# Second attention with its maps combined on VectorE, norm weights in the split, last transpositions among the projections, and zero products in four places

## The chip, the cores and the metric

The kernel runs on one core of a Trainium2 chip. The metric is the time of one execution on the device in microseconds (us); the median of several runs counts. Five engines work beside each other, each through its own queue of instructions in order: TensorE (PE: matrix products and transpositions), VectorE (DVE), ScalarE (ACT), GpSimd (POOL) and SyncE (SP), which here only issues DMAs. They wait for each other by semaphores.

## What is computed

Two transformer blocks on 256 tokens of width 1024 in float32. The change lies in the first half of the first block, whose second attention is a differential one: two softmax maps per head, the second subtracted with a weight, and a norm over each head's output:

```python
def _diff_attend(q, k, v, lam):
    s = jnp.einsum('bqhmd,bkhmd->bhmqk', q, k).astype(jnp.float32) * (HEAD_DIM ** -0.5)
    p = jax.nn.softmax(s, axis=-1)
    a = (p[:, :, 0] - lam * p[:, :, 1]).astype(v.dtype)
    return jnp.einsum('bhqk,bkhe->bqhe', a, v)

def _diff_out(o, subln, lam_init):
    o = _rmsnorm(o, subln, SUBLN_EPS) * (1.0 - lam_init)
    return o.reshape(o.shape[0], o.shape[1], B_WIDTH)

def _merge(ya, yb, ga, gb, w_oa, w_ob, w_out):
    merged = jax.nn.sigmoid(ga) * (ya @ w_oa) + jax.nn.sigmoid(gb) * (yb @ w_ob)
    return merged @ w_out

# in first_block, x: 256 tokens, ctx: 256 more keys and values
        ya = _sweep_query_blocks(_gqa_attend, qa, ka_all, va_all)
        yb = _sweep_query_blocks(lambda qq, kk, vv: _diff_attend(qq, kk, vv, lam), qb, kb_all, vb_all)
        yb = _diff_out(yb, subln_b[l], lam_init)
        x = x + g_a * _merge(ya, yb, ga, gb, w_oa[l], w_ob[l], w_out[l])
        ...
        x = x + g_m * moe(hx.reshape(b * s, d)).reshape(b, s, d)
```

There are 4 heads with two maps each, 512 keys, and a value width of 128; `lam_init` is 0.2, so the norm's weight is multiplied by 0.8. Attention A has 8 query heads over 2 key heads. `moe` has 32 experts of which each token takes four. The second block (three more attentions and a feed-forward layer) follows.

## The kernel before

**Products in float32.** A dense product is made of three fast ones: both operands are split into a high part, rounded to the fast format, and a low part, the rest. For weights `ensure_split` does it a quarter of a tile at a time: ScalarE writes `wh` (L316), VectorE writes `wl` (L319). `dense_tok` (L354 to L356) and `dense_feat` (L388 to L390) use them. `split_out` (L508) splits results for the next product, with an optional scale.

**Weights.** All weights come as tiles of 1 MB in one list; `fill` issues their DMAs on SP's queue as soon as a slot of the ring is free, `free` releases a slot when its last reader is done. In the first block the list also holds 16 tiles `("ada", g, k)` of the modulation's weights. `ada_one` (L659) multiplies such a tile with a column on VectorE and adds it up in `ga_b` and `gm_b` (L667 and L669); after eight tiles it has the sums over partitions made by TensorE (L676), copies them to `mrow` (L679) and transposes them (L682 and L689).

**Order.** The program is written as a foreground (the dense products, a quarter after the other) and a list `bg` of small tasks, of which `pump` runs some after each quarter: the norms of keys and queries, the steps of `attend_a` and `attend_b`. The compiler's scheduler then orders each engine's queue by its own estimates; so the order on an engine is not quite that of the text.

**First steps.** The modulation's first part is made by `ada_first` and `ada_second`: `mrow` (L640), two transpositions (L646), `mod` (L650), `ab`. With it `feat_norm` makes the normalised input `hi_t`, `lo_t` from transpositions of `xn` (L467); `warm` puts zero products between (L556).

**Attention A**, 16 units: scores (`mm3_pair`, L362), `soft` with exponential on ScalarE (L878) and a scaling by GpSimd (L900), `trans` (L910), product with the values (L922). It is spread over the projections `vb` and `g1`.

**Attention B**, 8 units of two maps each, over the projection `g1`: after the second map's exponential GpSimd multiplies it with 1/sum and -lambda (L962), VectorE scales the first and adds (L963), TensorE transposes (L971), multiplies with the values (L983), ScalarE copies the result to `va_sb` (L986). When all are done, `fin1` makes the norm: squares on ScalarE (L1007), sums (L1008), a reciprocal root in 13 small steps (`rsqrt`, L404 to L423), two multiplications by it (L1012) and two by the norm's weights `subln` (L1013), all on VectorE; `fin2` transposes (L1019) and splits into `yb`.

**Output.** The products with `w_oa` and `w_ob` (key `oab`, L1177 to L1179) take two quarters of `ya` and two of `yb` for each half; after the first quarter rows are spread over all partitions (`spreads`). Then `w_out` (`wo`), the residual `x_sb` (L1245), its transpositions for the router (L467), the router (L1233), the choice of experts on VectorE, and the experts (`expert_mm`, L1431) with up to 19 slots for their tiles. `keep_warm` (L447) puts products without use between.

## Time and profile before

| | us |
|---|---|
| median of 3 runs | 1687.87 (1687.73 to 1687.89) |
| profiled execution | 1689.61 |
| its span | 1687.7 |
| TensorE busy | 1627.8 (96%) |
| VectorE busy | 693.5 (41%) |
| ScalarE busy | 465.6 (28%) |
| GpSimd busy | 84.0 (5%) |

The profiled execution is one of its own; the durations come from it, and what lies outside its span is 1.9 us. By stage: the first 296 us are the first block's modulation, projections, attentions and router, with attention A from about 116 to 167 us and B from there to 217 us; from 296 to about 1240 us the experts; then the second block. A row of the timeline gives start, duration, engine, line, operation, written tile, read tiles, shape, and in brackets the idle time of the engine just before and what ended it. TensorE's clock is given as the share of 2.4 GHz that was granted.

### The profile page before, as it was taken

Reading aid. Unit: us, or ns where it says so; the run is one execution under the profiler, and the core shown is the slowest. Engines: PE = TensorE matmul, PEld = TensorE weight load, DVE = VectorE, ACT = ScalarE, POOL = GpSimd, SP = SyncE. Lnnn points to the kernel's source line nnn. Section 1 sums busy time; section 2 is a strip of 40 time slices with the busy share of each in tenths; the row PEclk is TensorE's granted clock in tenths of the full one; section 3 lists DMA queues with packets and bytes.
Section 4 is the critical chain, followed back from the end, with each engine's and each line's share of the span. In section 5 each row is a group of like instructions: output and inputs, shape, how many; then the busy total and the mean of one; then the engine's idle time right before and its main releaser. Section 6 shows DMA issues by size and latency. Waiting matters only on the chain. (4 is left out here: it accounts for less than half of the span.)

```text
span 1687.7 us, 22284 instructions
## 1 busy us (share of the span) xinstructions
PE 1627.8 (96%) x9091; PEld 1021.4 (61%) x9091; DVE 693.5 (41%) x1352; ACT 465.6 (28%) x769; POOL 84.0 (5%) x116
## 2 busy tenths in 40 slices
PE   8999999999999999899999999999999999999997
PEld 5877887444433443354344334434488899989996
DVE  4998986211111111121221111111367556665555
ACT  3435563101000100010001001000256445454443
POOL 3012200000000000000000000000004101100000
PEclk9999999999999999999999999999999999999999
DMA  9654669899999999999999999999973433565540
GB/s 380 240 193 157 203 243 371 368 425 426 425 425 425 425 425 426 384 425 425 426 425 426 425 425 426 426 408 425 405 291 108 142 123 128 179 217 183 174 158 25
DMA packets 117155, 537.29 MB, mean 318 GB/s; under 512 B 11882, under 2 KB 13622, under 8 KB 66874
## 3 DMA queue, kind: packets, MB, share of 16 engines
q1 hardware_dynamic: 112160, 532.19, 78.9%
q10 hardware_dynamic: 4458, 3.46, 0.6%
q8 instruction: 72, 1.18, 0.3%
q14 instruction: 33, 0.27, 0.0%
q0 software_dynamic: 432, 0.19, 0.0%
HBM read 534.75 MB, written 1.05 MB: 317 GB/s over the span
## 5 line engine op out<-in xcount | busy, mean ns | idle before, releaser
L1431 PE MATMUL bank_a<-w,xg 128*64 128x512 f32 x2048 | 521.9, 598 | 1.1 <-DMA w<-in_w_up_dram 1.1
L1431 PEld LDWEIGHTS bank_a<-w,xg 128*64 128x64 f32 x2048 | 184.7, 137 | 276.7 <-issue 254.0
L319 DVE TENSOR_TENSOR wl<-w,wh 128x1024 fp32r<-128x1024 f32 (+1 forms) x193 | 236.6, 1231 | 154.3 <-ACT wh L316 144.0
L316 ACT ACTIVATE wh<-w 128x1024 fp32r<-128x1024 f32 (+1 forms) x193 | 202.0, 1049 | 217.2 <-PE bank_a L389 88.2
L1431 PE MATMUL bank_a<-w,at 128*64 128x512 f32 x960 | 228.0, 595 | 6.2 <-DVE e L1462 5.3
L390 PE MATMUL bank_a<-hi,wl 128*128 128x256 f32 x640 | 180.3, 283 | 1.0 <-DVE wl L319 1.0
L388 PE MATMUL bank_a<-hi,wh 128*128 128x256 f32 x616 | 176.3, 287 | 1.1 <-ACT hi L474 0.6
L389 PE MATMUL bank_a<-lo,wh 128*128 128x256 f32 x616 | 174.3, 283 | 0.2 <-DVE lo L475 0.2
L1431 PEld LDWEIGHTS bank_a<-w,at 128*64 128x64 f32 x960 | 83.7, 137 | 145.6 <-issue 104.4
L513 ACT ACTIVATE y<-bank_a,ws 128x512 fp32r<-128x512 f32 x32 | 22.0, 688 | 441.6 <-PE bank_a L1431 431.7
L390 PEld LDWEIGHTS bank_a<-hi,wl 128*128 128x128 f32 x640 | 122.3, 192 | 1.4 <-DVE wl L319 1.4
L388 PEld LDWEIGHTS bank_a<-hi,wh 128*128 128x128 f32 x616 | 117.8, 192 | 3.2 <-issue 0.9
L389 PEld LDWEIGHTS bank_a<-lo,wh 128*128 128x128 f32 x616 | 118.1, 192 | 0.9 <-DVE lo L475 0.6
L514 DVE SCALAR_TENSOR_TENSOR y<-bank_a,ws,y 128x512 fp32r<-128x512 f32 x32 | 24.0, 751 | 217.1 <-ACT y L513 215.5
L1462 DVE TENSOR_SCALAR e<-bank_a 128x512 f32<-128x512 f32 x32 | 22.1, 691 | 187.3 <-PE bank_a L1431 185.7
L1452 ACT ACTIVATE e<-gs 128x512 f32<-128x512 f32 x32 | 20.2, 631 | 236.5 <-DVE gs L1451 224.9
L1341 PEld LDWEIGHTS bank_a<-gr,x_sb 128*128 128x128 f32 x512 | 65.1, 198 | 22.7 <-issue 19.5
L1451 DVE TENSOR_SCALAR gs<-bank_a 128x512 f32<-128x512 f32 x32 | 22.1, 692 | 134.4 <-PE bank_a L1431 114.1
L1341 PE MATMUL bank_a<-gr,x_sb 128*128 128x128 f32 x512 | 70.2, 289 | 0.2 <-DVE gr L1324 0.2
L1346 DVE TENSOR_SCALAR xg<-bank_a,abp 128x128 f32<-128x128 f32 x64 | 22.0, 404 | 107.8 <-PE bank_a L1341 107.6
L1349 ACT ACTIVATE xg<-bank_a,abp 128x128 f32<-128x128 f32 x64 | 24.3, 456 | 122.7 <-PE bank_a L1341 122.6
L354 PE MATMUL bank_b<-wh,hh 128*128 128x512 f32 x128 | 49.9, 390 | 0.0
(468 smaller groups left out, 2215.6 us busy)
## 6 DMA issues: line engine op xcount, KB each, us to landing
w<-in_w_up_dram SPq DMA_DIRECT2D x144, 1024.0 KB, 19.5
w<-in_w_down_dram SPq DMA_DIRECT2D x136, 1024.0 KB, 19.5
w<-in_w_gate_dram SPq DMA_DIRECT2D x128, 1024.0 KB, 18.5
w<-in_w_in_dram SPq DMA_DIRECT2D x44, 1024.0 KB, 7.4
w<-in_w_ada_dram SPq DMA_DIRECT2D x16, 1024.0 KB, 5.6
w<-in_w_ada_dram SPq DMA_DIRECT2D x16, 512.0 KB, 8.9
w<-in_w_out_dram SPq DMA_DIRECT2D x8, 1024.0 KB, 8.4
w<-in_w_down_dram SPq DMA_DIRECT2D x16, 512.0 KB, 10.9
```

The lines of the kernel that those rows point to most:

```text
L316: split_last[0] = S.activation(r32(wh[:, :n]), t[:, o:o + n], AF.Copy)
L319: V.tensor_tensor(r32(wl[:, :n]), t[:, o:o + n], wh[:, :n], op=OP.subtract)
L354: PE.matmul(o, r32(sh), r32(mh), start=first, stop=False)
L388: PE.matmul(o, r32(wh[:, k, c]), r32(hi[:, j]), start=j == 0 and m % 2 == 0, stop=False)
L389: PE.matmul(o, r32(wh[:, k, c]), r32(lo[:, j]), start=False, stop=False)
L390: PE.matmul(o, r32(wl[:, k, c]), r32(hi[:, j]), start=False, stop=j == 7 and m % 2 == 1)
L514: V.scalar_tensor_tensor(out=r32(lo), in0=src, scalar=scale, in1=hi, op0=OP.mult, op1=OP.subtract)
L1341: PE.matmul(ps[:, k], x_sb[:, tt, o:o + 255:2], d["gr"][:, tt].rearrange("p e s -> p (e s)"), start=tt == 0, stop=tt == 1)
L1349: S.activation(xg[:, j], ps[:, k], AF.Identity, bias=abp_[:, 1, j:j + 1], scale=abp_[:, 0, j:j + 1])
L1431: state["mm"] = PE.matmul(ps[h][64 * ab:64 * ab + 64], lhs(j, ab), w[ab][:, e, 512 * h:512 * h + 512], start=bias is None and j == 0, stop ...
L1451: V.tensor_scalar(out=g_, in0=ps[h], scalar1=7.0, scalar2=None, op0=OP.min)
L1462: V.tensor_scalar(out=u_, in0=ps[h], scalar1=7.0, scalar2=-7.0, op0=OP.min, op1=OP.max)
```

## The change

- **Attention B.** GpSimd's scaling is gone. With both sums known, VectorE takes the reciprocals of both at once and makes one column, -lambda times first sum over second sum; one operation over 512 columns adds the second map times this column to the first. The missing 1/(first sum) is the scale of ScalarE's copy of the product with the values. Squares are summed there too, per head and half of the tokens, by a ScalarE operation over 128 columns.
- **Its norm** is made in two parts: heads 0 to 2 in the last step but one, head 3 as the last task, each with its own 13 small steps. The weights `subln` are a column now, loaded as an 81st row of `rows` and turned with these; they are the scale in `split_out`.
- **Last transpositions** stand after the first quarter of `oab`, the spreads after the second.
- **Attention A** has two empty tasks more ahead of its first transposition, and 15 zero products (`warm_tile`) on TensorE just before it.
- **`ada_one`**: what follows the copy to `mrow` is a task of its own (`ada_rest`), at most one task later.
- **Zero products**: 16 instead of 8 at the start, 7 between two pairs of transpositions of `x_sb`, 14 instead of 8 ahead of the choice of experts.

```diff
-    def transposed(ps, j0, src):
-        for k in range(2):
-            for tt in range(2):
-                turned[tt] = PE.transpose(ps[:, k, 128 * tt:128 * tt + 128], src[:, tt, 128 * (j0 + k):128 * (j0 + k) + 128], ident)
+    def transposed(ps, j0, src, mid=None):
+        for k, tt in ((0, 0), (1, 0), (0, 1), (1, 1)) if mid else ((0, 0), (0, 1), (1, 0), (1, 1)):
+            if mid and (k, tt) == (0, 1):
+                mid()
+            turned[tt] = PE.transpose(ps[:, k, 128 * tt:128 * tt + 128], src[:, tt, 128 * (j0 + k):128 * (j0 + k) + 128], ident)
...
+        nc.gpsimd.dma_start(out=rows[80:81], in_=I["subln_b"])
...
+        def warm_tile(t, n, inst):
+            with tc.issue_after(inst.ins):
+                for _ in range(n):
+                    PE.matmul(t, zero_b[:, 0:128], zero_b, start=True, stop=True)
...
             V.tensor_copy(mrow, ps)
+            bg.insert(min(len(bg), 1), lambda: ada_rest(g, mrow))
+
+        def ada_rest(g, mrow):
             pt = bank("b", shape=(128, 4, 128))
...
-        warm(8, turned[1])
+        warm(16, turned[1])
...
                 pt = bank("b", shape=(128, 4, 128))
+                if u == 0:
+                    warm_tile(pt[:, 0:2].rearrange("p a n -> p (a n)"), 15, pair_last[0])
...
-            return [step(n) for n in range(21)]
+            return [step(n) for n in range(3)] + [lambda: None] * 2 + [step(n) for n in range(3, 21)]
...
-                    G.tensor_scalar(out=pr, in0=pr, scalar1=rl, scalar2=nlam, op0=OP.mult, op1=OP.mult)
-                    V.scalar_tensor_tensor(out=p0, in0=p0, scalar=r0, in1=pr, op0=OP.mult, op1=OP.add)
+                    p0 = st[u][1]
+                    V.reciprocal(rinv[:, u], mx[:, 2:6:3])
+                    V.scalar_tensor_tensor(out=mx[:, 6:7], in0=mx[:, 2:3], scalar=nlam, in1=rinv[:, u, 1:2],
+                                           op0=OP.mult, op1=OP.mult)
+                    V.scalar_tensor_tensor(out=p0, in0=pr, scalar=mx[:, 6:7], in1=p0, op0=OP.mult, op1=OP.add)
...
-                S.copy(late["sb"][:, qt, h], ps)
+                S.activation(late["sb"][:, qt, h], ps, AF.Copy, scale=rinv[:, u, 0:1])
+                S.activation(sqj, late["sb"][:, qt, h], AF.Square, accum_out=bss[:, h // 3, qt, h % 3:h % 3 + 1])
...
+            def norm(k):
+
+                n = (3, 1)[k]
+                hs = slice(3 * k, 3 * k + n)
+
+                def run():
+                    r = rsqrt(bss[:, k, :, 0:n], (2, n), 1.0 / 128, 1e-5)
+                    for qt in ((0, 1), (slice(0, 2),))[k]:
+                        y = late["sb"][:, qt, hs]
+                        rr_ = r[:, qt].unsqueeze(2 if k == 0 else 3)
+                        V.tensor_tensor(y, y, rr_.to_broadcast([128, n, 128] if k == 0 else [128, 2, n, 128]), op=OP.mult)
+                return run
...
-                    split_out(late["yb"][:, 0, :, s], late["yb"][:, 1, :, s], pt)
-                return run
-            late["fin"] = [fin2(0), fin2(1)]
-            return [step(n) for n in range(23)] + [fin1, lambda: None, late['fin'][0], late['fin'][1]]
+                split_out(late["yb"][:, 0, :, s], late["yb"][:, 1, :, s], pt, subln)
+            late["fin"] = fin2
+            tasks = [step(n) for n in range(23)]
+            tasks[21] = seq2(tasks[21], norm(0))
+            return tasks + [norm(1)]
...
-        subln = p1.tile([128, 128], F32, name="subln")
+        subln = p1.tile([128, 1], F32, name="subln")
...
+        V.tensor_scalar(out=subln, in0=cols[:, 96:97], scalar1=0.8, scalar2=None, op0=OP.mult)
...
             ada_one()
+        flush()
...
                 if (h, q) == (0, 0):
+                    late["fin"](0)
+                    late["fin"](1)
+                if (h, q) == (0, 1):
                     for f in spreads:
                         f()
...
-                    transposed(ps, 4 * h + 2 * b, x_sb)
+                    transposed(ps, 4 * h + 2 * b, x_sb, (lambda: keep_warm(7, turned[0])) if h and not b else None)
...
-        keep_warm(8, routed)
+        keep_warm(14, routed)
```

The scheduler moves instructions at more places than the text does. In the order listings below a row gives line, operation, written tile, read tiles and shape; lines of the changed kernel are 2 to 41 higher than those of before.

VectorE at the second half of `ada_first`, where `mod` (L650 before, L660 after) is waited for by TensorE's transpositions of `xn`. Before:

```order
L1053 TENSOR_TENSOR sgn<-rope,gains 128x32 x4
L1047 TENSOR_TENSOR cg<-rope,gains 128x128
L1053 TENSOR_TENSOR sgn<-rope,gains 128x32 x4
L650 TENSOR_TENSOR mod_232<-bank_b,cols 128x8 x2
L657 COPY ab<-mod_232 128x4 x2
L655 SCALAR_TENSOR_TENSOR ab<-mod_232,cols 128x4 x2
L319 TENSOR_TENSOR wl<-w,wh 128x1024
```

After:

```order
L1091 TENSOR_TENSOR sgn<-rope,gains 128x32 x4
L650 COPY mrow<-bank_b 128x256
L677 TENSOR_SCALAR ga_b<-w,ada_s 128x1024
L677 TENSOR_SCALAR gm_b<-w,ada_s 128x1024
L660 TENSOR_TENSOR mod_233<-bank_b,cols 128x8 x2
L667 COPY ab<-mod_233 128x4 x2
L665 SCALAR_TENSOR_TENSOR ab<-mod_233,cols 128x4 x2
L319 TENSOR_TENSOR wl<-w,wh 128x1024
```

The copy to `mrow` has come behind the rope's tables `cg` and `sgn`, and the first products of the ada tile (1, 0), which waits for its DMA, have come ahead of `mod`; before they stood after the next three splits `wl`.

TensorE where `mrow` of the first eight ada tiles is made, in attention A. Before:

```order
L390 MATMUL bank_a<-hi_t,wl 128x256
L676 MATMUL bank_b<-ga_b,ones 32x512 x2
L676 MATMUL bank_b<-gm_b,ones 32x512 x2
L682 MATMUL bank_b<-ident,mrow 128x128 x4
L689 MATMUL bank_b<-ident,mrow 128x128 x4
L910 MATMUL bank_b<-ident,pexp 128x128 x4
L362 MATMUL bank_b<-ka,qq 128x512 x4
```

After:

```order
L392 MATMUL bank_a<-hi_t,wl 128x256
L686 MATMUL bank_b<-ga_b,ones 32x512 x2
L686 MATMUL bank_b<-gm_b,ones 32x512 x2
L925 MATMUL bank_b<-ident,pexp 128x128 x4
L695 MATMUL bank_b<-ident,mrow 128x128 x4
L702 MATMUL bank_b<-ident,mrow 128x128 x4
L364 MATMUL bank_b<-ka,qq 128x512 x4
```

One group of four transpositions of attention A has come between the sums and the transpositions of `mrow`. On VectorE the first product of the next ada tile stands ahead of the copy to `mrow` both times.

TensorE at the last transpositions of attention B. Before:

```order
L388 MATMUL bank_a<-hi_t,wh 128x256
L389 MATMUL bank_a<-lo_t,wh 128x256
L390 MATMUL bank_a<-hi_t,wl 128x256
L1019 MATMUL bank_b<-ident,va_sb 128x128 x8
L1177 MATMUL bank_a<-ya,wh 128x256
L1178 MATMUL bank_a<-ya,wh 128x256
L1179 MATMUL bank_a<-ya,wl 128x256
```

After:

```order
L1215 MATMUL bank_a<-ya,wh 128x256
L1216 MATMUL bank_a<-ya,wh 128x256
L1217 MATMUL bank_a<-ya,wl 128x256
L1050 MATMUL bank_b<-ident,va_sb 128x128 x8
L1215 MATMUL bank_a<-ya,wh 128x256
L1216 MATMUL bank_a<-ya,wh 128x256
L1217 MATMUL bank_a<-ya,wl 128x256
```

They have moved behind 24 products of the first `oab` quarter. Ahead of these the 24 products of the last `g1` quarter stand between them and the last product with the values. On VectorE the split `wl` of the quarter after next stands just ahead of the norm of head 3 (13 small steps and one multiplication), and another one behind it, ahead of the two steps of `split_out`. At attention A's first transposition TensorE has, between the scores and the 15 zero products, 39 products of `g1` in a row; before it had none there.

## Rows read from the trace of the kernel before

**Rows 1.** Windows: stretch, length, busy us of PE, PEld, DVE, ACT, POOL; clock, DMA, GB/s.

```profile
30.00:50.00 20.00, 18.54 (x157) 14.04 (x156) 13.82 (x50) 8.04 (x14) 6.05 (x6) 1.00 1.04 412
50.00:118.97 68.97, 68.62 (x346) 56.16 (x345) 67.16 (x161) 28.32 (x47) 3.26 (x4) 1.00 0.49 175
118.97:221.60 102.63, 95.85 (x788) 81.64 (x788) 92.56 (x190) 58.05 (x122) 25.64 (x24) 0.98 0.64 214
295.00:299.50 4.50, 4.50 (x27) 1.88 (x27) 2.35 (x11) 1.71 (x3) 0.00 (x0) 1.00 0.02 5
300.00:650.00 350.00, 343.74 (x1568) 148.44 (x1566) 64.47 (x141) 33.19 (x64) 0.00 (x0) 1.00 1.01 424
121.97:125.38 3.41, 3.41 (x18) 3.41 (x17) 3.41 (x10) 1.96 (x6) 2.02 (x2) 0.50 1.06 441
224.37:231.20 6.83, 5.50 (x26) 5.53 (x27) 6.38 (x8) 4.17 (x6) 0.00 (x0) 0.50 0.78 272
289.22:292.63 3.41, 3.21 (x16) 2.57 (x14) 3.16 (x16) 0.15 (x1) 0.00 (x0) 0.50 1.02 417
```

**Rows 2.** The page's costliest group: the first two products of the experts.

```profile
L1431 PE MATMUL bank_a<-w,xg 128*64 128x512 f32 x2048 | 521.9, 598 | 1.1 <-DMA w<-in_w_up_dram 1.1
```

**Rows 3.** Waits of TensorE from 50 to 226 us: total, times, longest.

```profile
PE bank_b L1019 <- DVE va_sb L1013: 4.1, 1, 4.1
PE bank_b L910 <- POOL pexp L900: 2.1, 1, 2.1
PE bank_b L971 <- DVE mx L879: 1.9, 2, 1.4
PE bank_b L682 <- DVE mrow L679: 1.5, 1, 1.5
PE bank_b L971 <- DVE pexp L963: 1.2, 1, 1.2
```

**Rows 4.** Timeline of TensorE: the eight zero products near the start.

```profile
18.94 1.04 PE L556 MATMUL bank_b<-zero_b 128*128 128x256 bf16 x8
```

**Rows 5.** Timeline around `mod`: ScalarE, SyncE's queue, VectorE, TensorE.

```profile
41.29 1.06 ACT L316 ACTIVATE wh<-w 128x1024 fp32r<-128x1024 f32 x1 [3.16 <-DMA w<-in_w_in_dram]
...
29.68 2.98 SPq L132 DMA_DIRECT2D w<-in_w_in_dram  x2
32.75 1.02 SPq L132 DMA_DIRECT2D w<-in_w_ada_dram  x1
...
54.47 0.75 DVE L667 TENSOR_SCALAR gm_b<-w,ada_s 128x1024 f32<-128x1024 f32 x1
...
46.57 0.63 PE L467 MATMUL bank_a<-ident,xn 128*128 128x128 f32 x4 [0.31 <-DVE mod L650]
```

**Rows 6.** Timeline of TensorE at the transpositions of `mrow`.

```profile
152.40 0.63 PE L682 MATMUL bank_b<-ident,mrow 128*128 128x128 f32 x4 [1.53 <-DVE mrow L679]
152.87 0.64 PE L689 MATMUL bank_b<-ident,mrow 128*128 128x128 f32 x4
```

**Rows 7.** Waits of VectorE from 118 to 226 us, the longest: total, times, longest.

```profile
DVE pexp L963 <- POOL pexp L962: 3.7, 7, 0.7
```

**Rows 8.** Timeline of ScalarE and VectorE at the norm of attention B.

```profile
218.62 1.06 ACT L316 ACTIVATE wh<-w 128x1024 fp32r<-128x1024 f32 x1 [0.68 <-PE bank_a L389]
...
219.72 1.22 DVE L319 TENSOR_TENSOR wl<-w,wh 128x1024 fp32r<-128x1024 f32 x1 [0.26 <-ACT wh L316]
...
222.05 0.17 DVE L422 TENSOR_TENSOR rs_t<-rs_t,rs_m 128x8 f32<-128x8 f32 x1
...
223.66 1.29 DVE L1012 TENSOR_TENSOR va_sb<-va_sb,rs_y 128x512 f32<-128x512 f32 x2
```

**Rows 9.** Timeline of TensorE: two products of the gate projection in a row.

```profile
220.92 0.28 PE L390 MATMUL bank_a<-hi_t,wl 128*128 128x256 f32 x1
221.04 0.28 PE L388 MATMUL bank_a<-hi_t,wh 128*128 128x256 f32 x1
```

**Rows 10.** Timeline of TensorE at the choice of experts.

```profile
288.95 0.18 PE L1296 MATMUL bank_b<-sel_b,kh 128*128 128x32 bf16 x1 [0.87 <-PE bank_b L447]
```

64 lines of the change are left out of this document (33 added, 31 removed).

## The prediction

> **What bounds the kernel now.** I read the page first: TensorE (PE) is busy nearly throughout, so a gain must come from its waits, from products that are not needed, or from stretches at half clock. The windows by stage [rows 1] show three regimes. From 300 us on, the experts run with the DMA engines at a share of 1.01 and 424 GB/s; TensorE waits only 1.1 us for the largest group of weights [rows 2], but no weight can come sooner than the queue brings it. Just before, from 295 to 299.5 us, the DMA moves 5 GB/s: all slots are full and the first expert product must free one. So whatever TensorE gains before 299.5 us moves the start of the expert stream by as much, and the 1388 us behind it shift along unchanged; whatever is changed inside the stream is not touched here. I therefore only add up what moves ahead of 299.5 us. The second reading is the waits of TensorE there [rows 3]: 4.1 us for the last transposition, 2.1 us for the first transposition of attention A, 1.9 and 1.2 us in attention B, 1.5 us for the row `mrow`. The third is the clock: three stretches at a granted 0.50 (1.2 instead of 2.4 GHz) in the places that the change works on, of 3.41, 6.83 and 3.41 us [rows 1]; in each TensorE had just waited or run small products. At half clock work takes twice as long, so such a stretch costs half its length where TensorE has work: 1.7, 3.4 and 1.7 us. The fourth is VectorE (DVE): busy 67.2 of 69.0 us in 50 to 119 us, and 92.6 of 102.6 us in 119 to 221.6 us [rows 1]. It is nearly a second bound.
>
> All terms below are changes of the profiled execution (1689.61 us, span 1687.7 us); since they are differences I take them off the median of the runs, 1687.87 us. About 0.2% (3.4 us) is what a measurement can tell from no change.
>
> **Zero products at the start, and the order of VectorE behind them (+3.2 us).** The eight added products fill a wait before the first projection. Eight of them take 1.04 us [rows 4]; they stand in idle time and cost nothing. They may keep the clock up there, but that gain cannot pass 47 us, because of an order that the diff does not show: VectorE now makes `ga_b` and `gm_b` out of the tile ada(1,0) before `mod`, where it made them about 8 us after it. When does this tile land? The queue issues two `w_in` tiles at 29.68 us, then the ada tile at 32.75 us [rows 5]. ScalarE waits for the first of the three until 41.29 us [rows 5], and the DMA moves 412 GB/s here [rows 1], so a tile of 1.05 MB takes 2.5 us and the ada tile lands about 46.3 us (an estimate from these rows). The two products take 0.75 us each [rows 5], so `mod` starts at about 47.8 us, and TensorE's second group of transpositions, which waited for `mod` until 46.57 us [rows 5], starts at about 48.0 us: 1.45 us later, however early TensorE came. It then stands idle from 46.26 (or sooner, if it comes earlier) to 48.0 us, 1.7 to 3 us. After 2.1 us of idle at 121 us the clock fell [rows 1, 3], after 1.5 us at 152 us it did not (the mean of 0.98 of 119 to 221.6 us [rows 1] is that one stretch alone), so I take one more stretch at half clock, 1.7 us. Bounds: 0 if the tile lands 1.5 us sooner than estimated, 4.9 us if the stretch is of the double length, as that at 224 us. From 50 us on TensorE has next to no waits, so the loss stays.
>
> **First transposition of attention A (-2.1 us).** It now stands behind 39 products of the gate projection, so the 2.1 us wait [rows 3] is filled with work that had to be done anyway, and the half-clock stretch at 121.97 us that followed should go: 2.05 and 1.7 us. Just ahead of it stand 15 zero products, at 0.11 us (1.04/8 and less in a row) some 1.65 us, which TensorE now pays, as the data is ready by then. Bounds: -0.4 (the stretch stays) to -3.7 (the products hide in some other wait).
>
> **`mrow` and its transpositions (-0.5 us).** The diff puts them one task later. In the order that results, only one group of four transpositions stands between. Such a group takes 0.47 us (152.40 to 152.87) [rows 6]; the rest of the 1.53 us remains, since on VectorE `ga_b` still stands ahead of the copy. The second `mrow` had no wait. Bounds 0 to -1.5.
>
> **Attention B (-2.0 us, and +0.5 us).** VectorE waits 3.7 us in seven places for GpSimd's scaling [rows 7], and TensorE 1.9 + 1.2 = 3.1 us in three for what comes out of it [rows 3]. The scaling goes; a small VectorE step (0.2 us, spacing of the small steps in [rows 8]) and a scale inside ScalarE's copy take its place. The eight reciprocals saved pay for the eight small steps. I take two thirds, since one of the waits is for the reciprocal of the maximum's chain, which stays. Bounds 0 to -3.1. The squeeze: TensorE's share of 119 to 221.6 us falls by some 6 us, to about 96.5, while VectorE still has 92.6: new queueing is likely, 0 to 3 us. In 50 to 119 us, where it is as tight, TensorE was idle for 0.35 of 68.97 us [rows 1], so I take 0.5.
>
> **Last transpositions (-7.5 us).** Now they stand behind one more quarter. From the last product with values TensorE has 24 products of the gate projection and 24 of the output projection, 0.12 us apart (220.92 to 221.04) [rows 9], 5.8 us, with the value product itself 6.6 us. The chain beside it begins when the quarter before ends: split on ScalarE 1.06 us, split on VectorE 1.22 us, 13 small steps at 0.20 us (eight between 222.05 and 223.66) 2.6 us, one multiplication of half the size of the two at 223.66 (0.65 us): 5.5 us with no latencies, some 5.9 with them [rows 8]. So it fits with 0.7 us to spare: the wait of 4.14 us and the stretch of 6.83 us at half clock both go, 4.1 + 3.4. Cover gone, each us of delay on VectorE is a us of wait. Bounds: -3.0 to -7.5. The output split needs `yb` only 4.7 us later (24 products and eight of the row spread), which covers its two steps on each engine.
>
> **Router (-1.0 us).** Seven products between transpositions and six more ahead of `strict_b` fill waits: TensorE stood idle 0.87 us before the latter [rows 10]. Six take 0.65 us, so they cost nothing. If the clock stays up through 289.22 to 292.63 us, only what follows 290.6 us is real work of TensorE: 1.0 us. Bounds 0 to -1.7.
>
> **The rest at nothing.** The scale by the norm's weights enters the split, as a scale that those steps take in the same time elsewhere; the column comes with rows that are turned anyway, one small DMA more on GpSimd's queue at the start, where the turned rows had no wait. Two squares over 512 columns become eight over 128 with a sum: about 2 us more of ScalarE, which is busy 58 of 102.6 us [rows 1].
>
> Sum: +3.15 - 2.1 - 0.5 - 2.0 + 0.5 - 7.5 - 1.0 = -8.45 us, so 1687.87 - 8.45 = 1679.4 us.
>
> **Rivals.** (B) The slow stretches move rather than vanish. Idle pieces of 0.5 to 1.5 us remain in the first 300 us, and each may bring one on. Price: 1.7 + 3.4 + 1.0 = 6.1 us given back, 1685.5 us. For it: the stretch at 289 us followed an idle time of only 0.9 us. Against it: three runs agree within 0.16 us, so these stretches come at the same places. The Trainium skill, TensorE: Matmul & The Clock Gate, Part 1 (The HAM clock gate), says that the gate judges activity on a time base of its own that no kernel restarts; by that rule a removed idle time does not secure a removed stretch, and 1685.5 us would be the likelier time. No run here yet shows which.
> (C) VectorE does not wait for the ada tile (it lands earlier), and attention B and the squeeze go as well as they can: 3.15 + 1.1 + 0.5 = 4.75 us less, 1674.6 us. Against it: the queue was full all along.
> (D) VectorE is the bound: B's waits stay, the squeeze costs 3 us, the last transpositions wait 1 us: 2.0 + 2.5 + 1.0 = 5.5 us more, 1684.9 us. For it: 92.6 of what will be 96.5 us. Both (B) and (D) give 1691.0 us, which is not to be told from no change.
> (E) Slower: the wait for the ada tile ahead of `mod` starts a chain. VectorE, idle there for 3.5 us, hands over each split late, TensorE waits at each and falls to half clock each time. The other terms give 11.6 us, so it decides from seven such stretches on (7 x 1.7 = 11.9 us) beside its own wait; with seven, 1687.87 - 11.6 + 1.45 + 11.9 = 1689.6 us. Against it: VectorE gets the two products out of the way early, and has 1.5 us less to do after.
>
> **How the numbers follow.** Forecast 0.55, (B) 0.13, (C) 0.14, (D) 0.09, (B) with (D) 0.05, (E) 0.04. The range 1674.5 to 1685.8 us leaves out half of (C), a third of (B), and the last two: 0.2. Faster by over 3.4 us are the forecast, (C) and nearly all of (B) and (D): 0.87; within it 0.09; slower 0.04.
>
> **What would show it.** After: `ga_b` ahead of `mod` with a DMA wait to about 46.3 us, and TensorE's wait for `mod` of 2 to 3 us; no wait at the first transposition of attention A, but 15 products of 0.11 us; 0.9 us left at `mrow`; VectorE without waits for GpSimd in attention B; no wait over 0.7 us at the last transpositions and no 0.50 there; the first slot that an expert product frees near 291 us instead of 299.5, and the DMA back at 425 GB/s from there to the end of the experts. Wrong would be: that slot earlier, but the end not by the same amount (the stream does not shift); or as many stretches at 0.50 as before.

## The result: slower, and not where the change works

The changed kernel takes 1698.66 us (median of four runs, 1698.06 to 1699.40) beside 1687.88 us for the kernel before: 1.0057 times as long, 95% interval 1.0045 to 1.0068. The forecast was 1679.4 us with a range of 1674.5 to 1685.8 us, so sign and size are wrong. The profiled execution of after took 1699.40 us, with a span of 1697.5 us. Executions of one kernel scatter by several us (e3 below: ten from 1680.60 to 1692.24 us), so a trace, which is of one execution, can lie off the median, and the ratios are not always those of the medians.

Two things differ from the forecast. The stretch ahead of the experts gave 0.3 us instead of 8.45: the first expert product starts at 295.64 us (before: 295.91). And the expert stage, which the forecast shifted along unchanged, is 10.7 us longer: its main loop's last product ends at 1206.87 us instead of 1196.41. Behind it both kernels run alike.

The windows of after, in the columns of [rows 1]: around `mod`, the projections, the two attentions, the experts, and two stretches at half clock.

```profile
30.00:50.00 20.00, 15.65 (x133) 11.18 (x131) 12.14 (x40) 6.71 (x10) 6.08 (x6) 1.00 1.04 392
50.00:123.19 73.19, 72.61 (x365) 60.03 (x365) 70.06 (x174) 30.29 (x53) 3.27 (x4) 0.98 0.50 177
123.19:227.52 104.33, 98.39 (x812) 83.69 (x812) 93.96 (x198) 60.88 (x134) 17.23 (x16) 0.98 0.65 211
300.00:650.00 350.00, 343.74 (x1578) 149.15 (x1575) 64.45 (x141) 33.17 (x64) 0.00 (x0) 1.00 1.01 419
51.19:54.60 3.41, 3.41 (x19) 3.41 (x18) 3.30 (x8) 1.40 (x3) 0.00 (x0) 0.50 1.01 387
157.00:160.41 3.41, 3.25 (x22) 2.92 (x23) 2.72 (x6) 1.66 (x6) 0.00 (x0) 0.50 0.69 262
```

The line to look at is the fourth. From 300 to 650 us TensorE is busy for the same 343.74 us as before and nothing waits longer, but the DMA moves 419 GB/s where it moved 424, at the same share of 1.01: its engines are as busy and carry 1.2% less. The same shows from 30 to 50 us, 392 instead of 412 GB/s. For 350 us this costs nothing, since nineteen slots of weights stand ahead of TensorE; the reserve only shrinks faster. It is called in later, where SP's queue pauses at a branch of the program (the test for overflow, near 675 us) and the DMA runs dry for a while. The worst four microseconds there, first of before, then of after:

```profile
696.00:700.00 4.00, 0.64 (x4) 0.18 (x5) 1.29 (x2) 0.60 (x1) 0.00 (x0) 0.85 0.39 127
700.00:704.00 4.00, 0.00 (x0) 0.00 (x0) 0.36 (x1) 0.00 (x0) 0.00 (x0) 0.89 0.36 147
```

TensorE's waits from 640 to 760 us (total, times, longest), before and then after, and for weights from 940 to 1200 us, again before and then after:

```profile
PE bank_a L1422 <- DVE gs L1451: 4.3, 1, 4.3
PE bank_a L1422 <- DVEq L1526: 2.0, 1, 2.0
```

```profile
PE bank_a L1463 <- PEq L1567: 5.8, 1, 5.8
PE bank_a L1463 <- DVE gs L1492: 5.6, 1, 5.6
```

```profile
PE bank_a L1431 <- DMA w<-in_w_down_dram: 0.9, 1, 0.9
PE bank_a L1472 <- DMA w<-in_w_down_dram: 3.7, 6, 1.4
```

By the same products in both traces, after is 2.2 us ahead at 672 us, 4.7 us behind at 732 us, 7.5 behind at 957 us and 10.4 behind at 1236 us. The waits at the branch are put down to VectorE or a sequencer, and the experiments below part them. The wait for the sequencer belongs to the changed order, which comes to the branch earlier: e3, with the faster DMA, waits for it as long (first line). The wait for `gs` goes with the late weights: it is 9.2 us in e1, which has the order of before and the slower DMA (second line), and e3 has none.

```profile
PE bank_a L1464 <- PEq L1568: 5.7, 1, 5.7
PE bank_a L1422 <- DVE gs L1451: 9.2, 1, 9.2
```

TensorE's waits of after up to 310 us; they answer [rows 3]:

```profile
PE bank_a L470 <- DVE mod L660: 3.6, 1, 3.6
PE bank_b L937 <- DVE pt L928: 1.8, 1, 1.8
PE bank_b L695 <- DVE mrow L689: 1.4, 2, 0.9
PE bank_b L925 <- POOL pexp L913: 1.2, 1, 1.2
PE bank_b L1003 <- DVE mxb L983: 1.0, 1, 1.0
```

The wait of 4.1 us for the last transposition is gone, those of attention B fell from 3.1 to 1.0 us, but `mod`, `pt` and GpSimd's `pexp` now make TensorE wait.

### The profile page after: what moved, and what is told of

Read it like the earlier page. It is cut to its first block, busy times and chain, and to the rows that moved or that the text cites. A ratio compares the mean times of both kernels' runs of the same rounds, so it can differ in the third digit from the quotient of the medians.

```text
span 1697.5 us, 22343 instructions
## 1 busy us (share of the span) xinstructions
PE 1632.7 (96%) x9127; PEld 1021.4 (60%) x9127; DVE 694.0 (41%) x1362; ACT 467.7 (28%) x783; POOL 76.1 (4%) x109
```

## What slowed the DMA: 32 bytes

Inside the expert stage the bytes of the two kernels are the same, and their orders too but for one product at 384 us, which is in favour of after (below). What the change does alter for the whole program is the size of one small tile: `cols` grew from 96 to 97 columns. It is allocated early, and the tiles behind it follow at the next multiple of 32 bytes, so everything allocated later moved up by 32 bytes in each partition, the slots for weights (8192 bytes per partition each) among them. Theory 1: a slot that doesn't start on a multiple of 256 bytes takes its weights more slowly. Rival: the order of work, or another part of the change.

Four kernels tell these apart. The two instruction orders remain as they were in before and in after; only widths change.

```diff
 e1, in the kernel before                       e2, in the changed kernel
-    cols = keep.tile([128, 96], F32, ...)     -    cols = keep.tile([128, 97], F32, ...)
+    cols = keep.tile([128, 97], F32, ...)     +    cols = keep.tile([128, 160], F32, ...)
-    V.tensor_copy(cols[:, 16:], ps[:, :80])   -    V.tensor_copy(cols[:, 16:], ps[:, :81])
+    V.tensor_copy(cols[:, 16:96], ps[:, :80]) +    V.tensor_copy(cols[:, 16:97], ps[:, :81])

 e3: e2, and ahead of the seven later slots; e4: this alone, in the kernel before
+    m1.tile([128, 56], F32, name="pad", tag="pad")
```

> The kernel before with nothing changed but the width of the tile cols: 97 columns of four bytes instead of 96, as in the changed kernel; the 97th is not used. The compiler then places every later tile 32 bytes higher in SBUF: the twelve ring slots for weights start 32 bytes behind a multiple of 256 instead of on one, the seven later slots 64 behind instead of 32. Theory 1 (the placing of the slots is what slowed the expert stream): 1697 to 1699 us, with the DMA at about 420 GB/s between 310 and 1000 us instead of 425. Rival (the slower stream comes from the changed order of work or from something else in the change): 1687 to 1689 us and 424 to 425 GB/s.

> The changed kernel with the tile cols widened to 160 columns, of which 97 are used as they were: later tiles move up by another 224 bytes, so that the ring slots start on a multiple of 256 again and the seven later ones 32 behind one, as in the kernel before. Theory 1 (placing): the stream is back at 424 to 425 GB/s and the time at 1684 to 1688 us; the stretch ahead of the first expert product perhaps 1 to 2 us shorter too, since the slower DMA also delayed the ada tile there. Rival (something else in the change): 1697 to 1700 us and 420 GB/s.

> As the run with cols at 160 columns, and a filler tile of 224 bytes ahead of the seven later slots, so that all nineteen slots for weights start on a multiple of 256. Theory 1 (each slot off a multiple costs its transfers some per cent): twelve slots moved off cost 10 us, so seven moved on should give back up to 6 us, 1679 to 1683 us, if the stage is still bound by the DMA then; at or above 427 GB/s. Rival (only some offsets cost, or the stage is no longer bound by the DMA at 425 GB/s): the same time as the run with cols at 160 columns, within 1 us.

> The kernel before with the filler tile of 224 bytes alone, so that its seven later slots start on a multiple of 256 as its ring slots do. Theory 1: up to 6 us faster, 1681 to 1684 us, above 425 GB/s in the expert stage. Rival (an offset of 32 costs nothing for these seven, or TensorE bounds the stage): 1687 to 1688 us.

Two more, in the kernel before, ask how coarse the grid is (`cols` at 112 and at 128 columns):

> The kernel before with the tile cols at 112 columns: the twelve ring slots start 64 bytes behind a multiple of 256, the seven later ones 96 behind. Theory 1a (any start off a multiple of 256 costs): as with 97 columns, 1697 to 1699.5 us, 419 to 420 GB/s. Theory 1b (a start on a multiple of 64 is good enough): 1687 to 1689 us and 423 to 425 GB/s, as the kernel before.

> The kernel before with the tile cols at 128 columns: the twelve ring slots start 128 bytes behind a multiple of 256, the seven later ones 160 behind. At 64 and 96 behind it was 1697.1 us and 419 GB/s. Theory 1a (any start off a multiple of 256 costs alike): 1696 to 1699 us, 417 to 420 GB/s. Theory 1c (a multiple of 128 is good enough): 1687 to 1689.5 us, 423 to 425 GB/s.

Offsets are those of the slots' addresses from a multiple of 256, as the compiler places the tiles (no trace shows an address); the rate is that of the window from 300 to 650 us.

| kernel | 12 ring slots | 7 later slots | GB/s | median us | ratio to before (95%) |
|---|---|---|---|---|---|
| before | 0 | 32 | 424 | 1687.88 | |
| after | 32 | 64 | 419 | 1698.66 | 1.0057 (1.0045 to 1.0068) |
| e1: before, 97 columns | 32 | 64 | 419 | 1699.46 | 1.0059 (1.0043 to 1.0076) |
| e8: before, 112 columns | 64 | 96 | 420 | 1697.07 | 1.0048 (1.0031 to 1.0065) |
| e9: before, 128 columns | 128 | 160 | 419 | 1697.92 | 1.0041 (1.0027 to 1.0056) |
| e2: after, 160 columns | 0 | 32 | 425 | 1685.19 | 0.9978 (0.9968 to 0.9987) |
| e4: before, all on the grid | 0 | 0 | 427 | 1686.11 | 0.9988 (0.9977 to 0.9999) |
| e3: after, all on the grid | 0 | 0 | 427 | 1681.23 | 0.9969 (0.9951 to 0.9987) |

(The kernel before took 1688.85 us in the runs beside e1 to e4, 1689.56 beside e8 and 1690.07 beside e9; ratios are taken within each group.) The windows from 300 to 650 us of e1, e2, e3, e4, e8 and e9, in this order:

```profile
300.00:650.00 350.00, 343.75 (x1569) 148.41 (x1567) 64.47 (x141) 33.12 (x64) 0.00 (x0) 1.00 1.01 419
300.00:650.00 350.00, 343.73 (x1578) 149.60 (x1576) 64.47 (x141) 33.23 (x64) 0.00 (x0) 1.00 1.01 425
300.00:650.00 350.00, 343.72 (x1576) 149.21 (x1572) 65.86 (x143) 33.23 (x64) 0.00 (x0) 1.00 1.01 427
300.00:650.00 350.00, 343.74 (x1568) 148.70 (x1565) 64.48 (x141) 33.24 (x64) 0.00 (x0) 1.00 1.01 427
300.00:650.00 350.00, 343.74 (x1569) 148.40 (x1567) 64.48 (x141) 33.12 (x64) 0.00 (x0) 1.00 1.01 420
300.00:650.00 350.00, 343.74 (x1568) 148.43 (x1566) 64.46 (x141) 33.17 (x64) 0.00 (x0) 1.00 1.01 419
```

Theory 1 stands. An unused 97th column alone makes the kernel before as slow as the changed one (e1), and 63 unused columns take the whole loss out of the changed one (e2). The rate follows the number of slots off the grid, in a straight line: none 427, seven 424 to 425, nineteen 419 to 420 GB/s. Seven of nineteen slots should cost 7/19 of 7.5, or 2.8 GB/s, and cost 2 to 3. Offsets of 64, 96, 128 and 160 cost the same as 32 (e8, e9): a multiple of 128 is not enough. So the kernel before was itself 2.7 us slower than need be (e4; its interval just excludes no gain), which is less than the 6 us that I had allowed. In its trace e4 is 2.3 us ahead of the kernel before when the experts begin, but not by the DMA, which moves 412 GB/s from 30 to 50 us in both. What differs there are, in the main, the stretches at half clock: the one at 23 us is missing, and the one at 225 us is 3.41 us long instead of 6.83. From there to 1170 us the faster stream gains another 4.4 us, and a stretch of 6.83 us at 1181 us, which the kernel before doesn't have, takes 2.8 of them back. That the offset costs is shown; why it does is not.

The Trainium skill, DMA: Bandwidth & Descriptors, section "How a descriptor splits into AXI transactions", says that a transfer which doesn't start on a multiple of 256 bytes has its first transaction begin at the multiple below it, and pays for the bytes ahead of its start. The direction agrees with the runs. By its figures (beats of 32 bytes, rows of 8192 bytes, hence 256 beats) the price would be an estimated 0.4% at 32 bytes and 1.6% at 128; the runs show 1.8% (427 to 419.5) at either, so the price doesn't grow with the offset, and the measurement decides.

## Why the first 296 us gave so little

Beside a kernel with the same slots the change as such is worth 1688.85 - 1685.19 = 3.7 us (e2 beside before) or 1686.11 - 1681.23 = 4.9 us (e3 beside e4, whose intervals overlap), not 8.45. Ahead of the experts the traces show 3.1 and 2.3 us of it. Another 2.0 us that were no part of the sum are gained inside the stage that the prediction had left out: in the first pair of experts a scatter product stood among the 16 products for the next pair, and the changed order has it behind them. Start, duration and count on TensorE, first of before, then of after:

```profile
382.18 1.88 PE L1431 MATMUL bank_a<-w,xg 128*64 128x512 f32 x4
383.99 0.49 PE L1517 MATMUL bank_b<-y,sc 128*128 128x512 f32 x1
384.42 3.65 PE L1431 MATMUL bank_a<-w,xg 128*64 128x512 f32 x12
```

```profile
381.90 3.65 PE L1472 MATMUL bank_a<-w,xg 128*64 128x512 f32 x16
```

Sixteen in one go take as long as twelve behind the break. All variants of the changed kernel gain these 2.0 us between 379 and 405 us, but the branch takes them back: e3 is 4.3 us ahead of e4 at 671 us, 0.6 us at 695 and 2.4 us at 1170 us. What it is ahead beyond that at the end (4.3 us) is the stretch at 1181 us, which e3 doesn't have. So what TensorE gains ahead of the branch does not simply shift the rest, as the forecast had it.

Ahead of the experts, by the same ends of work in before, after and e3 (the last product of the key and query projections, of the gate projection, of `wl` in the output projection, and the first expert product):

| step | before | after | e3 | after - before | e3 - before |
|---|---|---|---|---|---|
| start to end of the key and query projections | 118.08 | 123.19 | 119.36 | +5.11 | +1.28 |
| from there, attentions A and B, to the end of the gate projection | 103.48 | 104.33 | 103.78 | +0.85 | +0.30 |
| from there to the end of the output projection (last transpositions) | 25.69 | 18.75 | 18.75 | -6.94 | -6.94 |
| from there to the first expert product (router) | 48.66 | 49.37 | 49.39 | +0.71 | +0.73 |
| sum | | | | -0.27 | -4.63 |

Of the -4.63 us, 2.3 are no effect of the change, since e4 has them too (see above); beside e4, e3 gains 2.3 us here. The second row holds a stretch at half clock in before (at 122 us) and in after (at 157 us), and none in e3. What such a stretch costs there can be read from e2 and e3: TensorE does the same at the same times in both, within 0.03 us, from 50 to 153 us; then the clock falls in e2 and not in e3 (the same window, first of e2, then of e3):

```profile
154.55:157.96 3.41, 3.41 (x17) 3.41 (x18) 2.69 (x7) 0.79 (x4) 0.00 (x0) 0.50 0.28 109
154.55:157.96 3.41, 2.91 (x23) 2.70 (x24) 2.42 (x6) 0.79 (x4) 0.00 (x0) 1.00 0.30 115
```

Over the whole row e2 takes 104.49 us, 0.71 more than e3; the waits behind the stretch take up the rest. The kernel after, e2, e5, e7, e11 to e14 and e16 have one at 153 to 157 us, e3, e6, e10, e15 and e17 none in this row, so about 0.7 us of a difference between the two groups is the clock's (an estimate from this one pair).

**The attentions** are the missing 4 us. The row in two halves, up to the last product with the values of attention A and from there, first of before, then of e3:

```profile
118.08:167.65 49.57, 45.96 (x396) 37.47 (x396) 44.32 (x95) 27.47 (x59) 16.04 (x16) 0.97 0.53 192
167.65:221.56 53.91, 50.78 (x400) 44.58 (x400) 49.09 (x98) 31.34 (x64) 9.60 (x8) 1.00 0.74 231
119.36:174.34 54.98, 49.98 (x436) 40.85 (x435) 47.80 (x93) 28.11 (x58) 17.30 (x16) 1.00 0.54 193
174.34:223.14 48.80, 47.30 (x379) 41.60 (x379) 46.44 (x105) 32.91 (x76) 0.00 (x0) 1.00 0.79 242
```

TensorE's idle time (length less busy time) falls from 3.13 to 1.50 us in attention B's half and rises from 3.61 to 5.00 us in A's, where the 15 zero products add 1.80 us of busy time. So what attention B gave was lost in attention A. Theory 2: VectorE bounds the stage, so that a wait of TensorE that is taken away comes back elsewhere. In e3 it is busy for 14.10 of 14.10 and for 14.66 of 14.70 us of attention B (the third of the busy times); TensorE is busy for 13.12 and 14.70 us there too, so busy time alone does not decide:

```profile
181.50:195.60 14.10, 13.12 (x100) 10.71 (x100) 14.10 (x32) 10.28 (x23) 0.00 (x0) 1.00 0.42 145
195.60:210.30 14.70, 14.70 (x124) 13.55 (x123) 14.66 (x32) 11.70 (x32) 0.00 (x0) 1.00 0.88 210
```

All experiments from here on start from e3. First the parts of attention A, and the order at `mod`:

```diff
 e5: no zero products (e6: nor empty tasks)
-                if u == 0:
-                    warm_tile(pt[:, 0:2].rearrange("p a n -> p (a n)"), 15, pair_last[0])
 e6, besides
-            return [step(n) for n in range(3)] + [lambda: None] * 2 + [step(n) for n in range(3, 21)]
+            return [step(n) for n in range(21)]
 e7, in ada_one
+                    with tc.issue_after(last_ab[0].ins) if g == 1 else nullcontext():
                         V.tensor_scalar(out=acc, in0=w[:, o], scalar1=ada_s[:, j, 0:1], ...)
```

> The kernel with all slots aligned (1681.2 us), without the 15 zero products ahead of the first transposition of attention A; the two empty tasks stay. Theory: the 15 products take 1.8 us on TensorE's path and hide nothing, so the dense projections of this stage end 1.8 us earlier (221.3 us instead of 223.1) and the kernel takes 1679 to 1680 us. Rival: without them TensorE stands idle for about as long at the same place, or a stretch at half clock comes back (1.7 us): 1681 to 1683 us.

> The kernel with all slots aligned, without the 15 zero products and without the two empty tasks, so that attention A is arranged as in the kernel before. Theory (the rearranged attention A loses 1.6 us where the prediction had 2.1 us gained): the wait of 2.1 us for GpSimd and the half clock of 1.7 us come back, the zero products of 1.8 us and the new waits of 3.6 us go; the dense projections end at 221.5 us instead of 223.1 and the kernel takes 1679 to 1681 us. Rival (the rearrangement is worth its 2.1 us, and the loss lies elsewhere): 1682.5 to 1684 us.

> The kernel with all slots aligned, with the two products of the tile ada(1,0) held back behind the last column of mod, about where the kernel before had them. Theory: the wait of TensorE for mod falls from 1.2 us to near 0.3 us as before, and everything behind shifts by about 1 us: 1680 to 1680.8 us. Rival: the two products fall into the tightest part of VectorE's work a little later and cost there what was saved, 1681 to 1682.5 us.

e5: 1682.78 us (0.9956 of before, 0.9942 to 0.9970). The stage takes 103.27 us instead of 103.78: 1.8 us of zero products went, and a stretch at half clock came, which e3 doesn't have (about 0.7 us, as above). The rival was nearer:

```profile
155.11:158.52 3.41, 3.41 (x18) 3.41 (x18) 2.73 (x10) 0.79 (x4) 0.05 (x1) 0.50 0.18 70
```

e6: 1683.22 us (0.9976, 0.9960 to 0.9991). The stage is 3.2 us shorter (100.58), more than I expected, but the gain is lost right behind it, to a wait of 3.0 us for `yb` and a stretch at half clock of 3.41 us at 230 us; the experts begin at 291.26 us, as in e3 (291.28). VectorE is not late there: its norm ends at 222.2 us and the last transpositions at 223.9 us. It is ScalarE's order: its split of `yb` starts at 229.06 us, behind a split `wh` that waits 2.65 us for weights of `w_out` and behind copies of `ga_b` and `gm_b`, where e3 has it straight behind the transpositions. So the time is in the rival's range and the stage is as the theory had it; a kernel with attention A as before and `yb` split first was not run.

```profile
PE bank_b L1213 <- ACT yb L516: 3.0, 1, 3.0
```

e7: 1681.11 us (0.9960, 0.9946 to 0.9973). The projections end 2.3 us earlier, and the stage takes 105.79 us, 2.0 longer; the rival was right about the time. Of the 2.3 us, 1.1 are left at 145 us, behind a wait of 1.06 us at 119 us that e3 doesn't have, and 0.3 at the end, behind a stretch at half clock at 154 us. So about half of the earlier start was waited away in attention A, and the clock took some 0.7 us.

So TensorE's own work alone does not set the pace of the attentions. Three runs load and relieve VectorE in attention B, on four of the weight splits (1.22 us each), which nobody waits for soon:

```diff
 e10 (e12: together with e7)
-                V.tensor_tensor(r32(wl[:, :n]), ...)
+                (G if i in (28, 30, 32, 34) else V).tensor_tensor(r32(wl[:, :n]), ...)
 e11
+                for _ in range(2 if i in (28, 30, 32, 34) else 1):
                     V.tensor_tensor(r32(wl[:, :n]), ...)
```

> The kernel with all slots aligned, in which VectorE makes the same four weight splits twice (4.9 us more of VectorE in attention B, none of it in a step that anyone waits for soon). Theory 2 (VectorE bounds the stage): the dense projections of the stage end 3 to 5 us later, 1684.5 to 1686.5 us. Rival (TensorE and latencies bound it): within 1 us, 1680 to 1682 us.

> The kernel with all slots aligned (1681.2 us), with four of the weight splits that VectorE makes during attention B (1.22 us each) given to GpSimd, which has no other work there. Theory 2 (VectorE bounds the stage from 119 to 223 us, where it is busy for 94 of 104 us and its own waits make up most of the rest): the dense projections of that stage end 3 to 5 us earlier and the kernel takes 1676.5 to 1678.5 us. Rival (TensorE and the latencies between the engines bound it, as the prediction had it): the same within 1 us, 1680 to 1682 us, or slower if GpSimd is late with a split or slows VectorE down.

> All slots aligned, the four weight splits on GpSimd, and the two products of the tile ada(1,0) behind mod. Theory 2: what the earlier mod saved ahead of attention A (2.3 us up to 87 us in its own run) was lost in attention A, where VectorE is as tight; with VectorE relieved only in attention B, little of it comes through: 1675.5 to 1678.5 us. Rival: as the run with the splits on GpSimd alone, or behind it.

e11: 1688.93 us, 7.7 more than e3 (0.9998 of before, 0.9982 to 1.0014), more than Theory 2 had. From 182 to 245 us the same products fall 8.8 us further behind those of e3, but not all by VectorE: 1.7 us up to the end of the dense projections, where Theory 2 had 3 to 5, and 2.5 us with the last transpositions, which wait 0.6 us for VectorE's norm. So half of the 4.9 us of work on splits that are needed much later reached TensorE. The rest is the wait below and a stretch at half clock of 6.83 us behind it; as in e6, ScalarE's split of `yb` (at 238.12 us) stands behind a split `wh` and copies of `ga_b` and `gm_b`:

```profile
PE bank_b L1216 <- ACT yb L517: 4.4, 1, 4.4
```

e10: 1684.19 us (0.9968, 0.9954 to 0.9983), no gain: the expected 3 to 5 us are missing and the stage takes 106.0 us. The cause is in the durations of VectorE's other steps (count, busy us, mean ns), first of e3, then of e10, in attention B:

```profile
L995 DVE SCALAR_TENSOR_TENSOR pexp<-pexp,mxb 128x512 f32<-128x512 f32 x8 | 6.0, 748 | 0.0
L679 DVE SCALAR_TENSOR_TENSOR ga_b<-w,ada_s,ga_b 128x1024 f32<-128x1024 f32 x2 | 2.6, 1276 | 0.0
```

```profile
L995 DVE SCALAR_TENSOR_TENSOR pexp<-pexp,mxb 128x512 f32<-128x512 f32 x8 | 8.0, 998 | 0.1
L679 DVE SCALAR_TENSOR_TENSOR ga_b<-w,ada_s,ga_b 128x1024 f32<-128x1024 f32 x2 | 4.7, 2340 | 0.0
```

Two of these steps are about three times as long, and the timeline of e10 (start, duration) shows beside what: each starts just behind a split on GpSimd and ends about its own length after GpSimd does (182.50 + 2.39 = 184.89, and 182.68 + 2.77 = 185.45).

```profile
182.50 2.39 POOL L319 TENSOR_TENSOR wl<-w,wh 128x1024 fp32r<-128x1024 f32 x1 [9.56 <-ACT wh L316]
193.31 2.62 POOL L319 TENSOR_TENSOR wl<-w,wh 128x1024 fp32r<-128x1024 f32 x1 [8.42 <-ACT wh L316]
```

```profile
182.68 2.77 DVE L995 SCALAR_TENSOR_TENSOR pexp<-pexp,mxb 128x512 f32<-128x512 f32 x1
193.61 3.40 DVE L679 SCALAR_TENSOR_TENSOR ga_b<-w,ada_s,ga_b 128x1024 f32<-128x1024 f32 x1
```

So 4.9 us were taken from VectorE and 4.9 given back as longer steps: 2.0 and 2.1 here, and 0.8 behind another of the four splits, at 172 us (2.06 us for 1.28). VectorE's busy time in the stage is 94.17 us, as in e3 (94.24), so e10 does not test what a relief of VectorE is worth. The Trainium skill, SBUF — State Buffer, section "Who interferes with whom", states that a VectorE instruction with two inputs in SBUF contends with a GpSimd instruction that reads SBUF, for a shared pair of ports that only one of them holds at a time. The trace agrees, with the 2.77 and 3.40 us for 0.75 and 1.28. e12, the same with `mod` first, took 1683.21 us (0.9974): it begins the stage 2.7 us before e10, whose clock had fallen at 49 us, and takes 2.2 us longer in it, of which a stretch at half clock at 154 us is about 0.7.

Last, relief through ScalarE, which is busy for 30 of 43 us in attention B:

```diff
 e13, attention B                              e14, attention A
-    (S.copy if u % 2 else V.tensor_copy)(at_, pt)   -    G.tensor_scalar(out=pr, in0=pr, scalar1=rl, ...)
+    S.copy(at_, pt)                           +    S.activation(pr, pr, AF.Copy, scale=rl)
 e15: both.  e16: e15 with e7.  e17: e15, and in attention A's trans
-                if u % 2:
-                    V.tensor_copy(o, pt)
-                else:
-                    S.copy(o, pt)
+                S.copy(o, pt)
```

> The kernel with all slots aligned; the four copies of turned maps that VectorE makes in attention B (0.68 us each, 2.7 us) go to ScalarE, which makes the other four and is busy for 30 of 43 us there. Theory 2 (VectorE bounds attention B): the last product of the stage's dense projections ends 2 to 2.7 us earlier after the same start, the time is 1678.5 to 1679.5 us. Rival (latencies between the engines bound it): within 1 us of 1681.2 us, or slower by ScalarE's longer queue.

> The kernel with all slots aligned; the 16 scalings of attention A (1.09 us each on GpSimd) are made by ScalarE, as an activation with a scale of its own. Theory 3 (GpSimd holds attention A: its 1.09 us stand in each unit's chain, and VectorE's steps on two operands in SBUF are slowed while it runs, 1.34 us instead of 1.27): the waits of 1.2 us for GpSimd and 1.8 us for pt go, VectorE gets back 1 us; 2 to 4 us earlier, 1677.5 to 1679.5 us. Rival (ScalarE, busy for 33 of 62 us, becomes the chain's end with 10 us more): 1681 to 1683 us.

> Both: the copies of attention B and the scalings of attention A on ScalarE. Theories 2 and 3: the gains add up, 1675 to 1677.5 us. Rival: no better than the better of the two alone.

> The kernel with the copies of attention B and the scalings of attention A on ScalarE (1678.9 us), and the two products of the tile ada(1,0) held back behind mod. Theory 2 (the start gained ahead of attention A was lost in it because VectorE is as tight there): some of it comes through now, 1676.5 to 1678.5 us. Rival (attention A takes as long as its chain takes, and an earlier start only waits longer): 1678.5 to 1680 us.

> The kernel with the scalings of attention A and the copies of attention B on ScalarE (1678.9 us), and the eight copies of turned maps of attention A that VectorE makes (0.68 us each) on ScalarE too. Theory 2b (TensorE waits 1.8 us for pt because the copy stands behind the steps that follow the row mrow on VectorE): that wait goes or falls under 0.5 us, 1676 to 1677.5 us. Rival (ScalarE is then the end of the chain, with 5.5 us more): the wait moves to a step of ScalarE, 1678.5 to 1681 us.

| kernel | median us | ratio to before (95%) | the stage, us | half clock in it |
|---|---|---|---|---|
| e3 | 1681.23 | 0.9969 (0.9951 to 0.9987) | 103.78 | none |
| e13 | 1681.94 | 0.9955 (0.9937 to 0.9973) | 103.29 | 3.41 us |
| e14 | 1680.35 | 0.9955 (0.9940 to 0.9970) | 102.65 | 3.41 us |
| e15 | 1678.93 | 0.9945 (0.9926 to 0.9964) | 100.67 | none |
| e16 | 1679.23 | 0.9941 (0.9925 to 0.9958) | 102.76 | 3.41 us |
| e17 | 1680.86 | 0.9954 (0.9938 to 0.9971) | 101.89 | none |

Each of the two reliefs shortens the stage by 0.5 and 1.1 us; without the stretches at half clock it would be 1.2 and 1.8 (an estimate with the 0.7 us of above), together 3.1. So they add up, but to less than the 4 to 6.7 us expected, and no time came as low as its theory had it. e15 is 0.55% faster than the kernel before; its interval overlaps that of e3, so only the stage in the trace separates the two. VectorE's busy time in the stage fell from 94.24 to 90.70 us by that, TensorE's is 97.13. Theory 2 is thus half borne out: VectorE's work reaches TensorE, by about half in e11 and by most of it in e15, but e15 also takes GpSimd out of attention A's chain, and no run parts the two. e16 and e17 bring nothing more, as their rivals said. In e17 the wait for `pt` goes over to ScalarE's copies (1.3 us); in e16 it stays with VectorE:

```profile
PE bank_b L938 <- DVE pt L929: 1.8, 1, 1.8
```

What that wait is can be read from e3's VectorE: behind the products that sum `ga_b` and `gm_b` it must write `mrow`, a split, `mod`, `abp`, the next two products of the ada tile and a maximum, and only then copies the turned maps that TensorE stands waiting for.

```profile
148.66 1.22 DVE L319 TENSOR_TENSOR wl<-w,wh 128x1024 fp32r<-128x1024 f32 x1
...
150.18 0.74 DVE L677 TENSOR_SCALAR gm_b<-w,ada_s 128x1024 f32<-128x1024 f32 x1
150.84 1.28 DVE L679 SCALAR_TENSOR_TENSOR ga_b<-w,ada_s,ga_b 128x1024 f32<-128x1024 f32 x1
152.04 0.69 DVE L888 TENSOR_REDUCE mx<-bank_b 128x1 f32<-128x512 f32 x1
152.64 0.68 DVE L928 COPY pt<-bank_b 128x512 f32<-128x512 f32 x1
```

Open remains why e15, e16 and e17 end the gate projection at 221.4 to 221.5 us although they begin the stage at 120.8, 118.8 and 119.5 us; e16's stretch at half clock is about 0.7 us of that.

## The prediction, point by point

**What bounds the kernel.** That the DMA bounds the experts from 300 us on was right as a reading, and wrong in what followed from it. "Whatever is changed inside the stream is not touched here" is the step that failed: the column of norm weights was costed at nothing ("the column comes with rows that are turned anyway"), since I looked at the instructions it adds and not at the bytes it takes. The tile it grew reaches the stream, and the stage is 10.7 us longer; so the sign of being wrong that the prediction names came, the first expert product earlier and the end not. No row of before shows an address; the share of 1.01 with a rate that could be compared between windows was the place to ask what sets the rate.

**The sum.** It is added up wrongly: its terms give -9.45 us, not -8.45, hence 1678.4 us, and the other terms of (E) are 12.6 us, not 11.6.

**Zero products at the start and `mod` (+3.15).** The order was read rightly. The estimate of 46.3 us for the ada tile is what e2 and e3 show, 46.29 and 46.31 us, and TensorE starts at 48.0 us as worked out (the rows are e2's):

```profile
46.29 0.75 DVE L677 TENSOR_SCALAR ga_b<-w,ada_s 128x1024 f32<-128x1024 f32 x1 [2.78 <-DMA w<-in_w_ada_dram]
48.01 0.63 PE L470 MATMUL bank_a<-ident,xn 128*128 128x128 f32 x4 [0.72 <-DVE mod L660]
```

In after itself the slower DMA brings the tile at 48.63 us, TensorE waits 3.56 us, and the stretch at half clock follows: +5.1 us. In e3 no stretch follows and the term is +1.3. So 1.45 us for the wait was right, and the 1.7 for the clock is a matter of the run.

**First transposition of attention A (-2.1).** The second step that failed. Its wait and its stretch at half clock went, and the 15 zero products cost 1.80 us (1.65 as written). What the sum left out is that the units behind it now meet GpSimd (1.2 us), ScalarE (0.6) and the queue behind `mrow` (1.8): the waits moved, and TensorE's idle time in attention A rose from 3.61 to 5.00 us (e3). e6 shows the same from the other side: with attention A as before the stage is 3.2 us shorter.

**`mrow` (-0.5).** 0.95 us remained at the first, as predicted; a second wait of 0.5 us came at the other one. Nothing gained.

**Attention B (-2.0, +0.5).** TensorE's waits fell by 2.1 us, VectorE's 3.7 us for GpSimd went, and TensorE's idle time in this half fell by 1.6 us, near the 1.5 of the two terms. The stage is no shorter because attention A took it. Rival (D), VectorE as the bound, came nearest in size for the first 296 us: its 5.5 us less gain would have given -3.0 us, e3 shows -4.6 beside the kernel before and -2.3 beside e4. In its mechanism it is half right: attention B's waits did go.

**Last transpositions (-7.5).** -6.9 (-6.1 beside e4), the one large term that came as worked out. They wait for nothing now (after):

```profile
230.19 1.04 PE L1050 MATMUL bank_b<-ident,va_sb 128*128 128x128 f32 x8
```

**Router (-1.0).** -0.9 from 282 to 296 us, and the stretch of 289 us is gone in after and e3, though e2, e5, e7, e10 and e13 have one at 283 to 288 us. But 1.6 us that no term had were lost ahead of it, at 250 to 256 us, of which waits for `wl` and `shb` show 1.0.

**The rivals.** (B) is half right: the three stretches of [rows 1] are gone, and after has two new ones, at 51 and 157 us; e3 has none between 28 and 600 us, e5 four. The rule cited there from the Trainium skill, TensorE: Matmul & The Clock Gate, Part 1 (The HAM clock gate), that the gate judges activity on a time base of its own, agrees with this: the same wait of 1.8 us, ending at 153.4 us, is followed by a stretch in e2 and by none in e3. (C) is out, since the tile landed at 46.3 us or later. (E), the slower case, was not it: no chain of stretches came from `mod`. What made it slower had no place among the cases, so no chance given to them could hold it.

## What to carry to other kernels

A tile that grows by one column moves every tile allocated behind it. Where a stage lives on DMA, compare the addresses of the buffers that the DMA fills, not only instructions and orders, and pad small tiles so that large buffers start on a multiple of 256 bytes. And a wait removed on one engine is only a gain if the engines that share its stage have time to spare (4.9 us more of VectorE's work cost TensorE 2.5 us in e11): read their queues over the whole stage before adding up the first one's waits. Where two traces of one order differ in their stretches at half clock, take that off before a difference is put down to an edit.

## What the hardware showed

- Weights that arrive in slots off a multiple of 256 bytes (all nineteen): 419 to 420 GB/s, on it 427, with the DMA engines at the same share of 1.01; offsets of 32 to 160 bytes cost alike.
- 5 GB/s less stayed hidden behind nineteen full slots (e1, in the order of before: 0.2 us behind at 671 us) and came out where the queue pauses (5.1 us behind at 702 us), then bit by bit up to 10.6 us at 1200 us.
- Behind a running GpSimd instruction of 2.4 to 2.6 us, VectorE's step on two operands in SBUF took 2.77 instead of 0.75 us and 3.40 instead of 1.28 us.
- The same work at the same times, within 0.03 us for 100 us, was followed by a granted clock of 0.50 for 3.41 us in one execution and of 1.00 in another (e2 and e3).
